# Hybrid encoder block on one core: the last group's two pairs of heads interleaved, their outputs staged in other tiles, modulation sums and FFN scalings placed sooner

## The chip, the cores and the metric

The kernel runs on one core of one Trainium2 chip, as one program. The metric is the device time of one execution in microseconds; the time before is the median of three runs. A core has TensorE (PE in the profile; PEld is its weight load), VectorE (DVE), ScalarE (ACT), GpSimd (POOL) and SyncE (SP). SP, ACT and POOL issue the DMAs.

## The reference

One layer of a bidirectional hybrid block on 256 tokens of width 2048, in fp32, and a final RMSNorm:

```python
mod = silu(c) @ ada_w + ada_b            # shift, scale, gate for the mixer (m) and for the FFN (f)
h   = rms_norm(x) * (1 + scale_m) + shift_m
proj = h @ w_in                          # all branches' inputs
h_a = mLSTM, both directions             # 4 heads, dk 256, dv 512
y_a = (sigmoid(a_o) * rms_norm(h_a)) @ w_branch_a
o_b = gated delta rule, both directions  # 16 heads of 128, behind a conv and l2 norms
y_b = (rms_norm(o_b) * silu(b_z)) @ w_branch_b
x = x + gate_m * ((g_a * y_a + g_b * y_b) @ w_out)
hf = rms_norm(x) * (1 + scale_f) + shift_f
x = x + gate_f * ((silu(gate) * up) @ w_down)     # gate, up = split(hf @ w_gate_up)
out = rms_norm(x) * norm_final_w
```

## The kernel before

Every weight matmul is done with operands split in a high and a low part (three products). ACT makes the high part (`wh`, L171 and L197), DVE the low part (`wl`, L172 and L198). `fjob` (out block of 128 channels) and `tjob` (tile of 512 channels, both token tiles t = 0 and 1) are generators; each `yield` ends a *piece* of 24 or 12 matmuls. The planner of the framework orders the instructions of each engine by its own cost estimates, with program order as priority; an instruction in `order(...)` keeps its place among its engine's instructions.

**Delta-rule stage.** The 16 heads are four groups g of four. For a group, `gdn_phase1` prepares each head, `gdn_invert` and `gdn_blocks` the triangular inverses, and `gdn_phase2(g, p)` finishes a pair p of heads in nine steps, each ended by `yield`: p1 (L717), p2 (L726), p3 (L739), p4 (L751), pa (L763/764, scaled by ACT into `z`), pb (L775, with `r` on DVE), pc (L763/764), po (L785 to L790, with the norm `gdn_norm`: squares on ACT L809, root L813, scaling into `on` on DVE L819), px (transposes of `on`, L796). At the end ACT copies px into `obt` (L798) and sends it to DRAM (`ob_d`, L799). `z` and `r` have one buffer, `on` and `pt` two. Between steps the loop draws pieces of other projections, by `fill` from the list `fills` (value and output gates `v`/`o`, the q and k blocks `a`, merge gates `ma`/`mb`), and for the next heads by `stream`. In group 3 no next heads are left, so every piece is a `fill`; `last` says how many follow each step. 23 pieces are left when the first pair of group 3 begins.

The tiles of this stage lie in the pool `bk`, among them `obt`. The pool `evp` holds evicted tiles of projections: `ev` and `evf` (two buffers of 128 x 256; `keep_f`, L339/L340, stores q and k blocks through it).

**What follows group 3.** `sx.close()` frees `bk`; in its place come `obh`/`obl` (the split delta outputs, L932/L933) and the pool `ml` of the mLSTM: per head the loads `mkq`, `vt`, `sgo` and `bc` on POOL (L937 to L944), and the last group's outputs (`o_load`, L886, POOL), which read `ob_d`. `psc` (L957) is the first matmul of an mLSTM head, `pden` (L981) and `ph` (L1002) follow. `y_b`'s first two pieces (`acc_yb`) use the first group's `obh`; its next two splits are held in program order behind the last group's.

**Modulation sums.** `ada_part` loads 1 MB of `ada_w` on SP (L126) and reduces it on DVE (L127); sixteen such sums and an addition (L129) make one part. `sums()` draws them from the list `background`; `pump()`, called once for every two pieces of a tile job, draws one for every `every[0]` calls. Parts 2, 3 and 4 run through the delta stage up to the output projection `o` (tiles g = 0 to 3), whose loop draws a sum after the listed pieces.

**FFN entry.** The last output tile is finished by token tile: `residual` (L1113 multiply and L1114 add on DVE, L1115 square on ACT), `token_rstd` (L1123, L1124, L1125). `normed(q, t, ...)` scales quarter q of token tile t into `xn` (L1191 on DVE, L1193 on ACT; two buffers of tag `sg`), `moved(b)` transposes block b (`pxn`, L1200), applies scale and shift (`hf`, L1204/L1206) and makes the high part (L1207), `low(b)` the low part (L1210). A loop over pairs of blocks alternates these with pieces of the first gate tile (`gt0`), twelve matmuls a pair of blocks.

Of the kernel before, what the change touches and what calls it, by code (L numbers as in the profile page):

```python
# [9 lines left out]
F32 = mybir.dt.float32  # L10
F32R = mybir.dt.float32r
AF = mybir.ActivationFunctionType
ALU = mybir.AluOpType
PSUM = bass.MemoryType.PSUM

P = 128
T = 256
# [35 lines left out]
def hybrid_block(ctx: ExitStack, tc: tile.TileContext, xr, nfr, crow, pk_d, cst_d, ada2, ada4, win0, winb, wint, wba, wbb, wo, wgu, wd, out, dbg=None):  # L53
    nc = tc.nc
    V, S, G, PE = nc.vector, nc.scalar, nc.gpsimd, nc.tensor

    def pool(stack, name, bufs=1, **kw):
        return stack.enter_context(tc.tile_pool(name=name, bufs=bufs, **kw))
# [27 lines left out]
    def order(ins, yes=True):  # L86

        return tc.keep_in_program_order(ins) if yes else ins
# [58 lines left out]
    count, every = [0], [0]  # L147
# [97 lines left out]
    def run(job):  # L245
        for _ in job:
            pass
# [3 lines left out]
    def fill(n=1):  # L251

        while n and fills:
            if next(fills[0], None):
                n -= 1
            else:
                fills.pop(0)
# [22 lines left out]
    evp = pool(sa, "evp", side="right")  # L280
# [3 lines left out]
    heads, parts = {}, {}  # L284
# [58 lines left out]
    def z_job(g, early=0):  # L343
        def done(ps):
            szs[g] = evp.tile([P, 2, 512], F32, tag="sz", bufs=1, name=f"sz{g}")
            for t in range(2):
                S.activation(szs[g][:, t], ps[t], AF.Silu)
        return tjob(f"z{g}", [wint[g, u] for u in range(4)], hh, hl, done, early)

    def b_job(h, j):  # L350
        return fjob(f"b{h}_{j}", winb[3 * (h - GRP) + j], lambda ps: gdn_conv(h, j, ps))
# [191 lines left out]
    bk = pool(sx, "bk")  # L543
# [161 lines left out]
    def gdn_phase2(g, p):  # L705
# [87 lines left out]
        for e, on in enumerate(ons):  # L793
            h, hl_ = 4 * g + 2 * p + e, 2 * p + e
            for t in range(2):
                PE.transpose(px[:, (2 * e + t) * P : (2 * e + t + 1) * P], on[:, t], ident)  # L796
            obt = bk.tile([P, T], F32, tag="obt", bufs=2, name=f"obt{h}")
            S.activation(obt, px[:, e * T : (e + 1) * T], AF.Copy, scale=pk[:, PK_GNW + h : PK_GNW + h + 1])  # L798
            S.dma_start(ob_d[g][hl_], obt)  # L799
        yield  # L800
# [35 lines left out]
    def stream(h0):  # L836

        todo = []

        def piece():  # L840

            for q in list(todo):
                q[0] -= 1
                if not q[0]:
                    todo.remove(q)
                    next(heads1[q[1]])

        for h in range(h0, min(h0 + 2, NH_B)):
            for j in range(3):
                for _ in b_job(h, j):  # L850
                    piece()
                    yield True
            todo += [[2, h], [4, h]]
        while todo:
            fill(1)
            piece()
            yield True
        while True:
            fill(1)
            yield True  # L860

    heads1 = {h: gdn_phase1(h) for h in range(NH_B)}
    after = (0, 1, 2, 1, 2, 2, 2, 2, 4, 0)
    last = (0, 1, 2, 1, 2, 2, 1, 1, 3, 0)


    for pair in ((0, 1), (2, 3)):
# [9 lines left out]
    def invert(g):  # L877
        gen = gdn_invert(g)
        next(gen)
        fill(4)  # L880
        for _ in gen:
            fill(1)

    def o_load(g, where, bufs):
        o4 = where.tile([P, 4, T], F32, tag="o4", bufs=bufs, name=f"o4_{g}")
        G.dma_start(o4, ob_d[g].rearrange("h p t -> p h t"))  # L886
        return o4

    o4s = []
    invert(0)  # L890
    for g in range(4):
        if g == 3:
            sf.close()
            op = pool(so, "op", side="right")
        blocks = gdn_blocks(g)
        next(blocks)
        fill(8)
        next(blocks)
        fill(1)
        pairs = [gdn_phase2(g, p) for p in range(2)]  # L900
        every[0] = (0, 2, 2, 2)[g]
        for p in range(2):
            pieces = stream(4 * g + 2 * p + 4)
            if g == 3:
                o4s += [o_load(i, op, 3) for i in ((0, 1), (2,))[p]]
            for n in range(1, 10):
                next(pairs[p], None)
                if p == 0:
                    next(blocks, None)
                for _ in range(after[n] if g < 3 else last[n]):  # L910
                    next(pieces)
            for _ in pairs[p]:
                pass

            if g < 3:
                while 4 * g + 2 * p + 5 not in heads:
                    next(pieces)
        if g < 3:
            fills.insert(0, z_job(g + 1))
            every[0] = 0  # L920
            invert(g + 1)
# [114 lines left out]
    def y_a(g, mgh, mgl):  # L1036
        gt = ml.tile([P, 2, 512], F32, tag="gt", bufs=2, name=f"gta{g}")
        nc.sync.dma_start(gt, ma_d[g])

        def done(ps):  # L1040
            c = slice(g * 512, (g + 1) * 512)
            for t in range(2):
                V.scalar_tensor_tensor(gt[:, t], gt[:, t], 1.0, ps[t], ALU.add, ALU.mult)
                V.tensor_tensor(mg[:, t, c], mg[:, t, c], gt[:, t], ALU.add)
            for e2 in range(2):
                px = gps(f"pxm{g}_{e2}")
                for e in range(2):
                    f = 2 * e2 + e
                    for t in range(2):
                        PE.transpose(  # L1050
                            px[:, e * T + t * P : e * T + (t + 1) * P], mg[:, t, g * 512 + f * P : g * 512 + (f + 1) * P], ident
                        )
                b = 4 * g + 2 * e2
                split(mgh[:, b : b + 2], mgl[:, b : b + 2], px.rearrange("p (e t) -> p e t", e=2))
        return tjob(f"ya{g}", [wba[g, u] for u in range(4)], hah, hal, done)
# [32 lines left out]
    mgh, mgl = big(bigC, F32R, "mgh"), big(bigC, F32R, "mgl")  # L1088
    for g in range(4):
        if g == 3:  # L1090
            every[0] = 0
            while len(background) > 2:
                sums()
            row_store(2, ml, 0.5)
        run(y_a(g, mgh, mgl))
    sm_.close()


# [29 lines left out]
    rs1 = xp.tile([P, 3], F32, name="rs1")  # L1128
# [23 lines left out]
    for g in range(4):  # L1152
        def done_o(*a, g=g):
            for t, ps in [a] if g == 3 else enumerate(a[0]):
                residual(t, g, ps, gm, ss1, wp, g == 3)
                if g == 3:
                    token_rstd(ss1, rs1, t)

        if g == 3:
            root()  # L1160
        between = (lambda: next(gt0)) if g == 3 else None
        for i, _ in enumerate(tjob(f"o{g}", [wo[g, u] for u in range(4)], mgh, mgl, done_o, by_token=between)):
            if i in ((4, 6, 7), (1, 2, 4, 6), (1, 2, 4, 6), (1, 2, 4))[g]:
                sums()
            if g == 3 and i == 4:
                sums(P)
                V.scalar_tensor_tensor(
                    affn, mod[:, 4 * KB : 5 * KB], 1.0, pk[:, PK_NFFN : PK_NFFN + KB], ALU.add, ALU.mult
                )
# [16 lines left out]
    def normed(q, t, parts, eng):  # L1186
        if q not in xns:
            xns[q] = hp.tile([P, 2, 512], F32, tag="sg", bufs=2, name=f"xn{q}")
        o, i = xns[q][:, t, parts], x1[:, t, q * 512 + parts.start : q * 512 + parts.stop]
        if eng is V:  # L1190
            order(V.tensor_scalar(o, i, rs1[:, t : t + 1], None, ALU.mult))  # L1191
        else:
            order(S.activation(o, i, AF.Copy, scale=rs1[:, t : t + 1]))  # L1193

    def moved(b):

        px = gps(f"pxn{b}")
        for t in range(2):
            f = b % 4 * P
            order(PE.transpose(px[:, t * P : (t + 1) * P], xns[b // 4][:, t, f : f + P], ident))  # L1200
        hfs[b] = hp.tile([P, T], F32, tag="hf", bufs=2, name=f"hf{b}")
        f, m = affn[:, b : b + 1], mod[:, 3 * KB + b : 3 * KB + b + 1]
        if b % 2 and b > 2:
            order(S.activation(hfs[b], px[:, 0:T], AF.Identity, scale=f, bias=m))  # L1204
        else:
            order(V.tensor_scalar(hfs[b], px[:, 0:T], f, m, ALU.mult, ALU.add))  # L1206
        order(S.activation(hfh[:, b], hfs[b], AF.Copy))  # L1207
# [5 lines left out]
    normed(0, 1, slice(0, 256), V)  # L1213
    for t in range(2):
        normed(0, t, slice(256, 512), S)
    moved(0)
    moved(1)
    low(0)
# [4 lines left out]
    for b in range(2, KB, 2):  # L1223

        next(gt0)
        low(b)
        low(b + 1)
        next(gt0)
        if b % 4 == 2 and b < 12:
            for t in range(2):  # L1230
                normed(b // 4 + 1, t, slice(0, 512), S)
        for e in (b + 2, b + 3):
            if e < KB:
                moved(e)
# [3 lines left out]
    for j in range(FB // 4):  # L1238
# [4 lines left out]
        for e2 in range(2):  # L1243
            px = gps(f"pxf{j}_{e2}")
            for e in range(2):
                f = 2 * e2 + e
                for t in range(2):
                    PE.transpose(px[:, e * T + t * P : e * T + (t + 1) * P], sg[:, t, f * P : (f + 1) * P], ident)
            b = 4 * j + 2 * e2
# [144 lines left out]
```

## Time and profile before

| | before |
|---|---|
| median of 3 runs | 1982.52 us (1982.24 to 1983.56) |
| profiled execution | 1979.27 us, span 1977.3 us |
| PE busy / PEld busy | 1918.9 us (97%) / 1705.5 us |
| DVE / ACT / POOL busy | 1402.5 / 1022.7 / 96.9 us |
| mean granted TensorE clock | 0.988 |
| DMA | 487.76 MB, mean 247 GB/s |

Times inside the profile are microseconds from the first instruction of the span. A row of the timeline gives start, length, engine, source line, operation, what it writes and reads, shapes, how many instructions were merged, and in brackets the idle time of the engine before it with what ended it. An engine name with a q is its queue issuing a DMA. The slices of the page cut the span into 40 parts of 49.4 us.

### The profile page before, as it was taken

To read this page: it belongs to the slowest core of one execution; us is meant where nothing else is said; L and a number is where in the kernel's file an instruction comes from. 1 tells how busy PE (TensorE), PEld (TensorE's weight loads), DVE (VectorE), ACT (ScalarE), POOL (GpSimd) and SP (SyncE) were. 2 spreads that over 40 slices of the span, in tenths; PEclk is the share of its full clock that TensorE was granted. 3 is DMA by queue.
4 is the path that set the end of the run, shared out by engine and by line. 5 is a ranking of instruction groups with operands and counts; after the bars stand their busy time and mean duration, and the time that the engine had idled before them with its cause. 6 is when DMAs were issued, how large, how long until landed. Compare 5 with 4: busy or idle time off the path is not lost.

```text
span 1977.3 us, 27036 instructions
## 1 busy us (share of the span) xinstructions
PE 1918.9 (97%) x10352; PEld 1705.5 (86%) x10352; DVE 1402.5 (71%) x2091; ACT 1022.7 (52%) x1568; POOL 96.9 (5%) x185
## 2 busy tenths in 40 slices
PE   8999999999999999999799999799999999999997
PEld 6887889989989998998688888688888888888886
DVE  5779887878988996965587769766666655555554
ACT  3146657855765686465454444554444444444443
POOL 0000300110100011000200000000000000000000
PEclk9999999999999999999799999899999999999999
DMA  9996665567667765885677679466766765566563
GB/s 400 420 383 194 222 223 192 167 203 283 228 199 247 281 214 191 310 303 190 234 291 266 249 288 419 182 234 235 265 244 237 262 246 193 205 240 203 202 206 114
DMA packets 78675, 487.76 MB, mean 247 GB/s; under 512 B 10265, under 2 KB 15681, under 8 KB 23889
## 3 DMA queue, kind: packets, MB, share of 16 engines
q1 hardware_dynamic: 63360, 450.95, 62.2%
q0 software_dynamic: 7872, 19.99, 4.4%
q10 hardware_dynamic: 7314, 15.10, 2.1%
q8 instruction: 81, 1.33, 0.3%
q14 instruction: 48, 0.39, 0.1%
HBM read 469.16 MB, written 16.83 MB: 246 GB/s over the span
## 4 chain that ended last, share of the span: by engine, by line
PE 73%; DVE 11%; DMA 9%; ACT 4%; issue 2%; POOL 0%; SPq 0%; ACTq 0%; DVEq 0%; POOLq 0%
DMA ra<-ada 5%; PE acc_up L215 4%; PE acc_up L218 4%; PE acc_up L216 4%; PE acc_d L216 4%; PE acc_d L215 4%; PE acc_d L218 4%; PE acc_gt L216 4%; PE acc_gt L215 4%; PE acc_gt L218 4%; PE acc_o L218 2%; PE acc_o L216 2%; PE acc_o L215 2%; PE acc_a L175 2%; PE acc_b L175 2%
## 5 line engine op out<-in xcount | busy, mean ns | idle before, releaser
L198 DVE TENSOR_TENSOR wl_d<-raw_d,wh_d 128x1024 fp32r<-128x1024 f32 x88 | 107.8, 1225 | 102.7 <-ACT wh_d L197 102.7
L127 DVE SCALAR_TENSOR_TENSOR ada<-ada,crow 128x2048 f32<-128x2048 f32 x64 | 146.5, 2289 | 43.6 <-DMA ada<-ada 43.5
L198 DVE TENSOR_TENSOR wl_up<-raw_up,wh_up 128x1024 fp32r<-128x1024 f32 x88 | 107.5, 1225 | 95.9 <-ACT wh_up L197 95.9
L197 ACT ACTIVATE wh_d<-raw_d 128x1024 fp32r<-128x1024 f32 x88 | 93.0, 1057 | 130.5 <-PE acc_d L216 125.3
L198 DVE TENSOR_TENSOR wl_gt<-raw_gt,wh_gt 128x1024 fp32r<-128x1024 f32 x88 | 107.7, 1224 | 72.4 <-ACT wh_gt L197 68.2
L197 ACT ACTIVATE wh_gt<-raw_gt 128x1024 fp32r<-128x1024 f32 x88 | 92.9, 1056 | 120.7 <-PE acc_gt L216 73.2
L197 ACT ACTIVATE wh_up<-raw_up 128x1024 fp32r<-128x1024 f32 x88 | 93.0, 1056 | 118.2 <-PE acc_up L216 71.7
L215 PE MATMUL acc_gt<-wh_gt,hfh 128*128 128x512 f32 x352 | 135.2, 384 | 0.0
L216 PE MATMUL acc_gt<-wh_gt,hfl 128*128 128x512 f32 x352 | 134.6, 382 | 0.0
L175 PE MATMUL acc_b<-hh,wh_b 128*128 128x256 f32 x576 | 134.6, 276 | 0.0
L175 PE MATMUL acc_b<-hl,wh_b 128*128 128x256 f32 x576 | 134.6, 277 | 0.0
L215 PE MATMUL acc_up<-wh_up,hfh 128*128 128x512 f32 x352 | 133.5, 379 | 0.0
L216 PE MATMUL acc_up<-wh_up,hfl 128*128 128x512 f32 x352 | 133.5, 379 | 0.0
L216 PE MATMUL acc_d<-wh_d,ffl 128*128 128x512 f32 x344 | 130.4, 379 | 0.0
L215 PE MATMUL acc_d<-wh_d,ffh 128*128 128x512 f32 x344 | 130.4, 379 | 0.0
L530 PE MATMUL first<-x,raw 128*128 128x256 f32 x512 | 114.5, 382 | 7.5 <-ACT x L523 6.8
L530 PEld LDWEIGHTS first<-x,raw 128*128 128x128 f32 x512 | 96.1, 190 | 25.9 <-ACT x L523 12.4
L175 PEld LDWEIGHTS acc_b<-hl,wh_b 128*128 128x128 f32 x576 | 110.6, 192 | 0.4
L175 PEld LDWEIGHTS acc_b<-hh,wh_b 128*128 128x128 f32 x576 | 110.5, 192 | 0.5
L197 ACT ACTIVATE wh_o<-raw_o 128x1024 fp32r<-128x1024 f32 x64 | 67.1, 1054 | 58.9 <-PE acc_o L216 35.5
L218 PE MATMUL acc_gt<-wl_gt,hfh 128*128 128x512 f32 x352 | 95.3, 385 | 0.0
L171 ACT ACTIVATE wh_b<-raw_b 128x1024 fp32r<-128x1024 f32 x72 | 76.1, 1058 | 37.1 <-PE acc_b L175 22.8
(384 smaller groups left out, 5018.4 us busy)
## 6 DMA issues: line engine op xcount, KB each, us to landing
ada<-ada SPq DMA_DIRECT2D x64, 1024.0 KB, 5.8
raw_gt<-wgu SPq DMA_DIRECT2D x44, 1024.0 KB, 5.0
raw_up<-wgu SPq DMA_DIRECT2D x44, 1024.0 KB, 4.9
raw_d<-wd SPq DMA_DIRECT2D x44, 1024.0 KB, 4.9
raw_b<-winb SPq DMA_DIRECT2D x36, 1024.0 KB, 5.0
ra<-ada SPq DMA_DIRECT2D x32, 1025.0 KB, 15.8
raw<-win SPq DMA_DIRECT2D x16, 1024.0 KB, 17.1
raw_z<-wint SPq DMA_DIRECT2D x16, 1024.0 KB, 5.2
```

The lines of the kernel that those rows point to most:

```text
L127: V.scalar_tensor_tensor(raw, raw, 1.0, row_c[:, :D], ALU.mult, ALU.mult, accum_out=mod[:, c0 + b : c0 + b + 1])
L171: S.activation(wh, raw[:, k0 : k0 + 8], AF.Copy)
L175: PE.matmul(o, wh[:, k], both(x, k0 + k).rearrange("p a b -> p b a"), start=k0 + k + i == 0, stop=False)
L197: order(S.activation(wh, raws[u][:, k0 : k0 + 2], AF.Copy), hold)
L198: order(V.tensor_tensor(wl, raws[u][:, k0 : k0 + 2], wh.bitcast(F32), ALU.subtract), hold)
L215: order(PE.matmul(ps[t], tok(xh, kk, t), turns(wh[:, k]), start=kk == 0, stop=False), early and steps > 1)
L216: PE.matmul(ps[t], tok(xl, kk, t), turns(wh[:, k]), start=False, stop=False)
L218: PE.matmul(ps[t], tok(xh, kk, t), turns(wl[:, k]), start=False, stop=kk == last)
L530: PE.matmul(first[o], raw[:, o], x[:, b], start=b == 0 and o % 2 == 0, stop=b == KB - 1 and o % 2 == 1)
```

## The change

- The outputs `obt` of all groups lie in `evp` under the tag `evf`, which they share with the q and k blocks, and no longer in `bk`.
- In group 3 the two pairs run in one loop of 13 steps: the first pair takes a step in each up to its end, the second from the fifth on, and two pieces are drawn in every step. Groups 0 to 2 run as before.
- `every[0] = 0` moves from the start of the last `y_a` tile to its end, so the counter draws sums there too. The `o` tiles draw 4, 4, 4 and 0 sums instead of 3, 4, 4 and 3.
- `normed` can also run on POOL. The second quarter is scaled there, ahead of the first transposes; the third and fourth are scaled on ACT at b = 4 and 8 instead of b = 6 and 10 (the second was at b = 2).

```diff
-            obt = bk.tile([P, T], F32, tag="obt", bufs=2, name=f"obt{h}")
+            obt = evp.tile([P, T], F32, tag="evf", bufs=2, name=f"obt{h}")
...
-    last = (0, 1, 2, 1, 2, 2, 1, 1, 3, 0)
...
-        for p in range(2):
+        for p in range(2) if g < 3 else ():
             pieces = stream(4 * g + 2 * p + 4)
-            if g == 3:
-                o4s += [o_load(i, op, 3) for i in ((0, 1), (2,))[p]]
...
-                for _ in range(after[n] if g < 3 else last[n]):
+                for _ in range(after[n]):
                     next(pieces)
...
+        if g == 3:
+            flow = [stream(4 * g + 4 + 2 * p) for p in range(2)]
+            for n in range(1, 14):
+                next(pairs[0], None)
+                if n > 4:
+                    next(pairs[1], None)
+                if n < 6:
+                    next(blocks, None)
+                if g == 3 and n in (1, 6):
+                    o4s += [o_load(i, op, 3) for i in ((0, 1), (2,))[n > 1]]
...
+                for _ in range(2):
+                    next(flow[n > 8])
...
     for g in range(4):
         if g == 3:
-            every[0] = 0
             while len(background) > 2:
                 sums()
             row_store(2, ml, 0.5)
         run(y_a(g, mgh, mgl))
+    every[0] = 0
...
-            if i in ((4, 6, 7), (1, 2, 4, 6), (1, 2, 4, 6), (1, 2, 4))[g]:
+            if i in ((2, 4, 6, 7), (1, 3, 5, 7), (1, 3, 5, 7), ())[g]:
                 sums()
...
-        if eng is V:
-            order(V.tensor_scalar(o, i, rs1[:, t : t + 1], None, ALU.mult))
+        if eng is not S:
+            order(eng.tensor_scalar(o, i, rs1[:, t : t + 1], None, ALU.mult))
...
+    for t in range(2):
+        normed(1, t, slice(0, 512), G)
     moved(0)
...
-        if b % 4 == 2 and b < 12:
+        if b % 4 == 0 and b < 12:
             for t in range(2):
                 normed(b // 4 + 1, t, slice(0, 512), S)
```

More of the change, by code (lines that the diff above doesn't have):

```diff
@@ L913, in hybrid_block @@
                 pass
-            if g < 3:
-                while 4 * g + 2 * p + 5 not in heads:
-                    next(pieces)
+            while 4 * g + 2 * p + 5 not in heads:
+                next(pieces)
+        if g == 3:
[8 more added lines that the diff above has]
+                    o4s += [o_load(i, op, 3) for i in ((0, 1), (2,))[n > 1]]
+                if n == 9 and g < 3:
+                    while 4 * g + 5 not in heads:
+                        next(flow[0])
+                for _ in range(2):
+                    next(flow[n > 8])
+            for pair in pairs:
+                for _ in pair:
+                    pass
+            while g < 3 and 4 * g + 7 not in heads:
+                next(flow[1])
         if g < 3:
```

## The prediction

> **What bounds the kernel now.** I read the page first, its busy shares and its slices.
>
> ```profile
> span 1977.3 us, 27036 instructions
> PE 1918.9 (97%) x10352; PEld 1705.5 (86%) x10352; DVE 1402.5 (71%) x2091; ACT 1022.7 (52%) x1568; POOL 96.9 (5%) x185
> PE   8999999999999999999799999799999999999997
> PEclk9999999999999999999799999899999999999999
> ```
>
> TensorE bounds: 58 us of the span are not its work, and the slices show two dips inside the kernel, one near 950 us and one near 1250 us; at both the granted clock dips too. Next the waits of TensorE, which say what ended them (total, times, longest):
>
> ```profile
> PE pxn L1200 <- ACT xn L1193: 11.6, 7, 6.8
> PE psc L957 <- DMA mkq<-kq_d: 3.7, 2, 3.3
> PE acc_yb L215 <- ACT obh L932: 3.5, 1, 3.5
> PE px L796 <- DVE on L819: 3.5, 2, 3.3
> PE pa L764 <- DVE UL L753: 2.8, 3, 1.2
> PE pb L775 <- DVE r L776: 2.3, 1, 2.3
> PE po L786 <- ACT z L768: 0.7, 1, 0.7
> PE px L796 <- ACT obt L798: 0.6, 1, 0.6
> ```
>
> All but the pa row lie in the two places that the diff edits: the end of the last group's second pair with what follows it, and the normalised activations of the FFN. The busy times by stage place them (columns: stretch, length, busy PE, PEld, DVE, ACT, POOL, granted clock, DMA share, GB/s):
>
> ```profile
> 858.00:932.30 74.30, 74.30 (x496) 69.33 (x495) 42.99 (x50) 45.31 (x86) 0.00 (x0) 1.00 0.67 237
> 932.30:946.00 13.70, 7.63 (x56) 6.84 (x54) 4.94 (x9) 7.28 (x21) 0.00 (x0) 1.00 0.55 193
> 966.50:980.10 13.60, 13.11 (x44) 11.31 (x43) 7.18 (x19) 6.20 (x10) 2.00 (x4) 0.50 0.47 158
> 1134.00:1169.00 35.00, 35.00 (x172) 30.83 (x171) 22.40 (x23) 15.52 (x18) 0.51 (x1) 1.00 0.65 228
> 1176.00:1225.00 49.00, 48.49 (x229) 42.26 (x228) 43.26 (x43) 22.94 (x29) 0.00 (x0) 1.00 1.01 420
> 1277.10:1280.50 3.40, 3.40 (x10) 2.65 (x9) 1.92 (x4) 2.23 (x4) 0.00 (x0) 0.50 0.00 0
> ```
>
> Up to 932.3 TensorE never idles in group 3: projection pieces cover both pairs. After it the pieces are gone, and the second pair's tail stands bare.
>
> **Part 1: the second pair four steps behind the first.** No arithmetic changes. The loop asks for 26 pieces (13 per pair before, 2 at each of 13 steps after), but only 23 are left: 7 of the last output gate, 8 of the last q/k blocks, 8 of the last merge gate. Before, the second pair had 10 of them, and by program order the last stood behind its step pc. The timeline shows how they went:
>
> ```profile
> 933.83 1.03 PE L218 MATMUL acc_ma<-wl_ma,hh 128*128 128x512 f32 x4
> 937.56 0.68 PE L775 MATMUL pb<-z,gg 128*128 128x128 f32 x4 [2.26 <-DVE r L776]
> 940.18 0.49 PE L786 MATMUL po<-z,at 128*128 128x128 f32 x2 [0.71 <-ACT z L768]
> 946.25 0.73 PE L796 MATMUL px<-cst,on 128*128 128x128 f32 x2 [3.34 <-DVE on L819]
> 947.54 0.69 PE L796 MATMUL px<-cst,on 128*128 128x128 f32 x2 [0.56 <-ACT obt L798]
> 948.77 0.33 ACTq L799 DMA_DIRECT2D ob_d<-obt  x1
> 950.66 2.95 ACT L932 ACTIVATE obh<-o 128x1024 fp32r<-128x1024 f32 x3 [1.92 <-DMA ob_d<-obt]
> 951.38 0.80 POOL L886 DMA_DIRECT2D o<-ob_d  x1 [100.38 <-DMA ob_d<-obt]
> 952.18 0.76 POOL L937 DMA_DIRECT2D mkq<-kq_d  x1
> 965.24 2.20 PE L957 MATMUL psc<-mkq 128*128 128x256 f32 x7 [3.33 <-DMA mkq<-kq_d]
> ```
>
> The last piece ended at 934.86, as pb began: two pieces earlier than in program order, so TensorE takes pieces ahead whenever a chain step is not ready. The bare tail holds 2.26 + 0.71 + 3.34 + 0.56 = 6.87 us of idle. Afterwards the pieces stretch, by program order, to one behind the second pair's po. If they again run two pieces ahead, the last one stands behind pc: the waits before pb and po go (2.97), the waits for the norm and for obt stay. I take **3.0**; ends 0 (they run out as early as now) and 6.9 (all covered). The total TensorE work is the same, so what is gained is idle time alone. Cover for the moved steps: the row 858 to 932.3, ACT 61% and DVE 58% busy. The two chains share z and r (one buffer each): the second pair's pa comes one step behind the first's po, so the wait falls away in program order. The two loads of earlier outputs stay at about the same pieces.
>
> **Part 2: obt in the evf tiles.** SP's gate load, ACT's obh and POOL's loads all started between 950.66 and 951.38, right after the last ob_d transfer landed: obt lay in the pool whose room obh, mkq, vt and the other tiles take. Without it the room is free when px has read on, at 948.23. obh and yb come up to 2.4 us earlier, but that alone is worth nothing, since TensorE then waits for mkq, and it is those landings that set psc, the decay products and the ph matmuls. POOL's load of the last outputs still needs ob_d. If POOL's later loads pass it, mkq issues at about 948.3 instead of 952.18: 3.9. If they stay behind it: 0. I take **3.2**, near the upper end, because the planned order lets ready work pass waiting work (here pieces passed pb). The load of the last outputs is then late next, by some four POOL issues (0.76 each); its user, yb's second chunk, is held far behind anyway. In the other direction obt can now wait for a q/k eviction's landing in the two evf buffers, with ACT's splits queued behind:
>
> ```profile
> kq_d<-ev_a ACTq DMA_DIRECT2D x4, 128.0 KB, 2.8
> ob_d<-obt ACTq DMA_DIRECT2D x4, 128.0 KB, 1.7
> ```
>
> One wait of at most 2.8 us on ACT, partly hidden by the split buffers: **-0.3**, ends -2.8 and 0. For groups 0 to 2 I count nothing, since the split buffers hide it; with that cover gone it is the same 2.8 us at most, once for each pair.
>
> **Part 3: the modulation sums.** Twelve sums are drawn in the first three output tiles and none in the fourth; before, three of 14 fell in the fourth. Two move into the last y_a tile (the counter now stays on there). On SP their loads of 1 MB queue among those of y_a's weights, where the DMA share is 0.65, and two such loads leave the stretch from 1176 on, where it is 1.01. In the last output tile two sums stood between the steps that TensorE waits for:
>
> ```profile
> 1253.12 0.59 PE L241 MATMUL acc_o<-wl_o,mgh 128*128 128x512 f32 x2
> 1251.77 2.28 DVE L127 SCALAR_TENSOR_TENSOR ada<-ada,crow 128x2048 f32<-128x2048 f32 x1
> 1253.98 0.69 DVE L1114 TENSOR_TENSOR x<-x,tmss 128x512 f32<-128x512 f32 x1
> 1257.37 2.28 DVE L127 SCALAR_TENSOR_TENSOR ada<-ada,crow 128x2048 f32<-128x2048 f32 x1
> 1257.48 0.63 ACT L1115 ACTIVATE tmss<-x 128x512 f32<-128x512 f32 x1 [1.54 <-DVE x L1114]
> 1260.51 1.97 PE L1200 MATMUL pxn<-cst,xn 128*128 128x128 f32 x8 [6.79 <-ACT xn L1193]
> 1266.48 1.32 ACT L1193 ACTIVATE xn<-x,rs 128x512 f32<-128x512 f32 x2
> 1275.75 0.33 PE L1200 MATMUL pxn<-cst,xn 128*128 128x128 f32 x1 [1.72 <-ACT xn L1193]
> ```
>
> The last matmul ended at 1253.71. From there, without sums: some 0.2 to start, multiply and add at 0.69 each, the square some 0.75, and then what now lies between the second sum's end (1259.6) and the first transpose (1260.5), 0.9 for the reduction, root, reciprocal and first scaling. That is 1257.0 to 1257.1 instead of 1260.51: **3.4**. Ends 1.4 (only the second sum leaves the path: it ends at 1259.6, the square before it at 1258.2) and 4.6 (both lengths). The two sums in y_a cost **-0.5**, ends -4.6 (both sums ahead of splits, 2.28 each) and 0: in the last y_a tile and on (1134 to 1169) TensorE has no idle and DVE is 64% busy, which hides them; with that cover gone it is their whole length.
>
> **Part 4: the scalings.** The second block of four goes to POOL ahead of the transposes, the third and fourth are issued two blocks sooner. Waits before pxn after the first: 11.6 - 6.8 = 4.8 us. With xn there, the next limit is ACT's queue: two pairs of scalings, 1.32 each, still stand in it ahead of the conversions that the matmuls need. I leave one such pair, 1.3 of the 4.8, as idle: **3.5**, ends 2.2 (both) and 4.8. POOL's scaling is not in the trace; its nearest rows are memsets:
>
> ```profile
> L552 POOL MEMSET cc<- 128x512 f32 x6 | 2.9, 521 | 5.7 <-DMA raw_v<-wint 5.7
> L552 POOL MEMSET UL<- 128x2048 f32 x1 | 1.8, 1795 | 0.0
> ```
>
> I take 1.3 us for one, between 0.52 and 1.8. The second starts at about 1257 and ends by 1258.8 at the latest; its reader comes after eight transposes and twelve matmuls (1.97 for the former, 1.03 for four of the latter), past 1261. So its price is 0. [...]
>
> **The clock.** In 1277.1 to 1280.5 the clock was 0.50 with TensorE busy throughout, behind the 1.72 us wait at 1275.75: half of 3.4, **1.7**, comes back if those waits go; ends 0 and 1.7. For the first transposes I count nothing: a gap of 3.4 us remains, and the 1.72 us wait was enough here. [...]
>
> **Sum.** 3.0 + 3.2 - 0.3 + 3.4 - 0.5 + 3.5 + 1.7 = 14.0 us. The profiled execution took 1979.27 us (span 1977.3), so 1965.3; the median of the runs, 1982.52, is 3.25 above it, and my number for it is **1968.5**.
>
> **Rivals.** *Early exhaustion (B):* the pieces run out as now and POOL's order stays. Group 3 gives nothing; 14.0 - 6.2 = 7.8 remain: 1974.7. For it: pieces already ran two ahead. Against it: now two pieces stand behind every step of the second pair, where one stood behind four of them. *Sums replaced (C):* another unordered DVE operation, a weight split say, takes the sums' place between the residual steps, and the scalings only move their wait: 1.4 + 1.5 instead of 3.4 + 3.5 + 1.7, so 14.0 - 5.7 = 8.3: 1974.2. *Full cover (D):* 6.9 and 3.9 in group 3, and the clock stays up where it was 0.50 from 966.5 to 980.1 (13.11 busy; some 5 us of it in long matmuls comes back): 14.0 + 3.9 + 0.7 + 5 = 23.6: 1958.9. *Slower (E):* with both chains in flight the planned order misjudges them, and TensorE is held at a chain step while ready pieces queue behind. The row of pa shows 1.2 us at the longest in earlier groups; at 13 steps that is 15.6 us, from which the other terms (14.0 - 3.0 = 11.0) are taken: 4.6 slower, 1987.1. It decides from 11.0 / 13 = 0.85 us a step. Against it: the row 858 to 932.3 has no idle with one chain. *Does not do what it says (F):* group 3 and the FFN both find a next waiter of the same length, and only the clock's 1.7 comes: 1980.8.
>
> **Chances.** My forecast 0.47, B 0.18, C 0.12, D 0.10, E 0.06, F 0.07. Below about 0.2% (4 us) a measurement of this kernel can't tell a change from none. Faster: the first four less 0.04 of B and C that would end within that bound, 0.83; same 0.11; slower 0.06. The range leaves out E, F and half of D: 1959 to 1979.
>
> **What would show it.** Group 3: pieces of acc_ma still running behind the second pair's pb; waits before pb and po gone; obh starting within 1 us of the last px; mkq issued ahead of the load of ob_d. FFN: no L127 between the last acc_o and the first pxn, that gap near 3.4 us, POOL's two scalings ended before 1261 on the old scale, no 0.50 stretch behind them. Wrong if L127 or L198 still stands there, if the psc waits grow by what yb gains, or if waits at p, pa or pb appear between 860 and 930.

## The result and the profile after

| | before | after |
|---|---|---|
| median of 5 runs each | 1983.56 us (1982.24 to 1986.4) | 1965.06 us (1961.58 to 1971.78) |
| ratio of times, 95% interval | | 0.9908 (0.9892 to 0.9923) |
| profiled execution, span | 1979.27, 1977.3 us | 1965.06, 1963.2 us |

The change is faster by 18 us (0.9%); the forecast was 1968.5, in a range of 1959 to 1979. The profiled executions differ by 14.2 us: that of before lay below its median, that of after is its median. Four executions among the experiments (two of the kernel before, one each of two changed kernels) took 2868 to 10526 us, in a slow state, and stand in no ratio below. The page of the changed kernel:

```profile
span 1963.2 us, 27039 instructions
...
PE 1915.5 (98%) x10352; PEld 1701.3 (87%) x10352; DVE 1400.6 (71%) x2091; ACT 1021.8 (52%) x1566; POOL 100.2 (5%) x187
...
PE   8999999999999999998999999999999999999997
...
PEclk9999999999999999999999999999999999999999
```

The busy time of every engine is the same within 5 us, so what was gained is waiting and clock: both dips of before, near 950 and near 1250, are gone from the clock's slices. Three rows of the timeline mark the stages, each the first matmul of one: the last branch projection (`acc_ya`), the output projection (`acc_o`) and the last of the FFN's eleven up tiles (`acc_up`). Before:

```profile
1076.19 0.38 PE L215 MATMUL acc_ya<-wh_ya,hah 128*128 128x512 f32 x1
1169.02 0.38 PE L215 MATMUL acc_o<-wh_o,mgh 128*128 128x512 f32 x1
1717.34 0.38 PE L215 MATMUL acc_up<-wh_up,hfh 128*128 128x512 f32 x1
```

After:

```profile
1067.62 0.38 PE L215 MATMUL acc_ya<-wh_ya,hah 128*128 128x512 f32 x1
1161.89 0.38 PE L215 MATMUL acc_o<-wh_o,mgh 128*128 128x512 f32 x1
1703.18 0.38 PE L215 MATMUL acc_up<-wh_up,hfh 128*128 128x512 f32 x1
```

Up to `acc_ya` 8.6 us were won (parts 1 and 2); `acc_ya` itself takes 92.8 and then 94.3 us, 1.4 more (part 3's price); from `acc_o` to `acc_up` 7.0 us were won (parts 3 and 4); behind that nothing. TensorE's waits after:

```profile
PE pxn L1216 <- ACT xn L1209: 3.5, 1, 3.5
PE acc_yb L218 <- DVE wl_yb L198: 3.1, 2, 2.5
...
PE px L796 <- DVE on L819: 2.4, 1, 2.4
...
PE acc_ya L218 <- DVE wl_ya L198: 1.9, 3, 1.1
PE acc_ma L215 <- ACT ev_a L339: 1.5, 1, 1.5
...
PE acc_gt L215 <- ACT hfh L1223: 1.2, 3, 0.4
```

Seven waits before `pxn` (11.6 us) have become one (3.5), those before `psc` (3.7) are down to 0.6, that for `obh` (3.5) is gone, that before `pb` too. New are `acc_ma`, behind ACT's eviction of a q/k block, `acc_yb`, and `acc_gt` behind `hfh`. The end of group 3 in the timeline of the changed kernel:

```profile
918.61 0.49 PE L786 MATMUL po<-z,at 128*128 128x128 f32 x2 [0.72 <-ACT z L768]
...
923.69 0.50 PE L796 MATMUL px<-cst,on 128*128 128x128 f32 x2 [2.35 <-DVE on L819]
...
924.75 0.69 PE L796 MATMUL px<-cst,on 128*128 128x128 f32 x2 [0.56 <-ACT obt L798]
...
926.15 0.81 POOL L953 DMA_DIRECT2D mkq<-kq_d  x1 [72.91 <-ACT obt L798]
...
926.46 0.38 ACT L339 ACTIVATE ev_a<-acc_a 128x256 f32<-128x256 f32 x1 [0.51 <-DMA ob_d<-obt]
...
926.89 0.79 PE L215 MATMUL acc_ma<-wh_ma,hh 128*128 128x512 f32 x1 [1.45 <-ACT ev_a L339]
...
927.45 1.06 ACT L948 ACTIVATE obh<-o 128x1024 fp32r<-128x1024 f32 x1 [0.61 <-ACT ev_a L339]
...
930.61 0.39 ACT L339 ACTIVATE ev_a<-acc_a 128x256 f32<-128x256 f32 x1 [2.10 <-DMA ob_d<-obt]
...
933.36 1.97 PE L973 MATMUL psc<-mkq 128*128 128x256 f32 x8 [0.17 <-issue]
...
936.08 0.76 POOL L885 DMA_DIRECT2D o<-ob_d  x1 [0.86 <-DMA sgo<-o_d]
```

The last px ends at 925.44 (before: 948.23). That is not 23 us gained: the last merge gate (`acc_ma`, 96 matmuls), which ran from 910.18 to 934.86 among the second pair's steps, now runs from 926.89 to 955.04, behind them. Its first matmul waits for an eviction `ev_a`, which frees an accumulator, and the first two of the four `ev_a` wait for landings of `obt`, with which they now share the two evf buffers (the other two, at 933.49 and 938.69, wait for the landings of the first two). The first `ev_a` of these four stood at 888.83 before. The 30 us behind the last px, by busy times (columns as in the prediction's windows), first before, then after:

```profile
948.23:978.23 30.00, 22.26 (x77) 18.07 (x77) 14.49 (x29) 10.92 (x15) 10.77 (x18) 0.67 0.73 254
```

```profile
925.44:955.44 30.00, 27.94 (x119) 23.61 (x120) 21.27 (x30) 17.81 (x22) 10.25 (x17) 0.90 0.97 332
```

TensorE is busy 27.9 us of 30 instead of 22.3, at a mean clock of 0.90 instead of 0.67: the merge gate covers the landings of the mLSTM's loads.

### The profile page after: what moved, and what is told of

Same layout as the page of the kernel before. It is cut to its first block, busy times and chain, and to the rows that moved or that the text cites. A ratio compares the mean times of both kernels' runs of the same rounds, so it can differ in the third digit from the quotient of the medians.

```text
span 1963.2 us, 27039 instructions
## 1 busy us (share of the span) xinstructions
PE 1915.5 (98%) x10352; PEld 1701.3 (87%) x10352; DVE 1400.6 (71%) x2091; ACT 1021.8 (52%) x1566; POOL 100.2 (5%) x187
## 4 chain that ended last, share of the span: by engine, by line
PE 71%; DMA 10%; DVE 10%; issue 4%; ACT 3%; POOL 0%; ACTq 0%; SPq 0%; DVEq 0%; POOLq 0%
PE acc_up L216 4%; PE acc_up L215 4%; PE acc_up L218 4%; PE acc_d L216 4%; PE acc_d L215 4%; PE acc_d L218 4%; PE acc_gt L216 4%; PE acc_gt L215 4%; PE acc_gt L218 4%; DMA ra<-ada 4%; PE acc_b L175 3%; PE acc_o L218 3%; PE acc_o L216 2%; PE acc_o L215 2%; DMA ada<-ada 2%
## 5 line engine op out<-in xcount | busy, mean ns | idle before, releaser
L127 DVE SCALAR_TENSOR_TENSOR ada<-ada,crow 128x2048 f32<-128x2048 f32 x64 | 146.5, 2289 | 56.2 <-DMA ada<-ada 56.1
L197 ACT ACTIVATE wh_o<-raw_o 128x1024 fp32r<-128x1024 f32 x64 | 67.1, 1054 | 57.7 <-PE acc_o L216 34.6
```

Source lines behind the costliest of these rows:

```text
L127: V.scalar_tensor_tensor(raw, raw, 1.0, row_c[:, :D], ALU.mult, ALU.mult, accum_out=mod[:, c0 + b : c0 + b + 1])
L197: order(S.activation(wh, raws[u][:, k0 : k0 + 2], AF.Copy), hold)
```

## The experiments

All ratios are to the kernel before, run beside each on the same chip; 0.001 is 2.0 us. Intervals of ±0.0015 are 3 us, so the difference of two changed kernels is uncertain by some 4 us, and by 5 where the intervals are ±0.0022.

| kernel | ratio (95%) | last px ends | `acc_ma` runs | last `acc_yb` ends |
|---|---|---|---|---|
| before | 1 | 948.2 | 910 to 935 | 1076.4 |
| after | 0.9908 (0.9892 to 0.9923) | 925.4 | 927 to 955 | 1067.8 |
| `obt` in evf alone | 0.9955 (0.9941 to 0.9969) | 936.9 | 917 to 963 | 1068.6 |
| interleaving alone | 0.9977 (0.9965 to 0.999) | 940.2 | 918 to 942 | 1074.6 |
| sums alone | 0.9997 (0.9978 to 1.0015) | 948.9 | 912 to 936 | 1078.9 |
| scalings alone | 0.9974 (0.996 to 0.9988) | 950.2 | 909 to 934 | 1079.2 |
| evf and interleaving | 0.9921 (0.9899 to 0.9942) | 923.6 | 925 to 953 | 1064.3 |
| before, `obt` in ev | 1.0048 (1.003 to 1.0067) | 950.9 | 939 to 962 | 1091.0 |
| after, `obt` in ev | 0.9938 (0.9916 to 0.996) | 945.9 | 923 to 948 | 1079.8 |
| after, head 12 alone in evf | 0.9933 (0.9918 to 0.9949) | 929.8 | 925 to 955 | 1067.0 |
| after, six steps behind | 0.9949 (0.9934 to 0.9964) | 946.3 | 914 to 939 | 1076.5 |
| after, two steps behind | 0.993 (0.9917 to 0.9943) | 925.3 | 928 to 956 | 1070.7 |
| after, scaling on ACT | 0.9899 (0.9877 to 0.9921) | 925.4 | 927 to 955 | 1066.8 |
| after, no sums in the last `y_a` | 0.9903 (0.9885 to 0.9922) | 924.0 | 926 to 954 | 1064.8 |

The times in the last three columns are of one profiled execution each, and such executions of one kernel differ by some us (that with all of `obt` in ev holds a wait of 4.4 us in an earlier group, below); the ratios are over all runs.

**The four parts, each alone.** The first two theories were the prediction's own: theory 1, the interleaving covers the second pair's tail and `obt`'s place matters little; theory 2, the gain is the room that `obt` leaves in `bk`, which lets the mLSTM's loads start at once.

```diff
-            obt = bk.tile([P, T], F32, tag="obt", bufs=2, name=f"obt{h}")
+            obt = evp.tile([P, T], F32, tag="evf", bufs=2, name=f"obt{h}")
```

> The kernel before with obt in the evf tiles and nothing else changed. Theory 1 (the gain in group 3 comes from the two chains ending sooner, with pieces of the last merge gate left behind them to cover the norm and the mLSTM loads): within 2 us of before, since the second chain ends as late as before and mkq's landing is all that can move. Theory 2 (the gain comes from the room of bk being free 2.4 us sooner and the loads passing the one that waits for ob_d): 4 to 8 us faster.

Measured: 0.9955, about 9 us, the largest of the four. Theory 1 missed it. Behind the last px in this kernel:

```profile
936.91:966.91 30.00, 27.47 (x115) 23.31 (x115) 22.30 (x30) 18.23 (x22) 10.25 (x17) 0.89 1.00 363
```

With the old loops, TensorE is as busy there (27.5 us of 30) as in the changed kernel; no wait for `mkq` at `psc` is left. But three of the four `ev_a` also come late, at 939.01, 942.50 and 948.52, which theory 2 does not speak of. A third theory came from this row, *held back*: what counts is that the shared buffers hold the q and k evictions, so that the merge gate's matmuls run behind the last px, where they cover the landings.

```diff
-        for p in range(2):
+        for p in range(2) if g < 3 else ():
...
+                next(pairs[0], None)
+                if n > 4:
+                    next(pairs[1], None)
```

> The kernel before with the two pairs of group 3 in one loop of 13 steps, obt still in bk. Theory 1: 5 to 8 us faster, px of the second pair some 20 us earlier than 948. Theory 2: 0 to 2 us faster, since obt's landing still holds the room.

Measured: 0.9977, some 4.6 us. Here px ends 8 us sooner than before and no step of either pair waits over 0.25 us from 860 on, more than part 1 promised; but behind px the time is given back:

```profile
PE psc L974 <- DMA mkq<-kq_d: 9.1, 2, 7.8
```

```profile
940.15:970.15 30.00, 17.44 (x61) 13.18 (x60) 15.74 (x23) 10.92 (x13) 9.88 (x17) 0.77 0.85 312
```

The merge gate ran among the chains (918 to 942), and TensorE has 17.4 us of work in the next 30. A matmul that fills a gap ahead of px is missing behind it.

```diff
-            every[0] = 0
             while len(background) > 2:
...
-            if i in ((4, 6, 7), (1, 2, 4, 6), (1, 2, 4, 6), (1, 2, 4))[g]:
+            if i in ((2, 4, 6, 7), (1, 3, 5, 7), (1, 3, 5, 7), ())[g]:
```

> The kernel before with the modulation sums moved alone. If the two sums between the residual steps were the price: the gap before the first pxn falls from 6.8 to 3.4 us and the run is 2 to 3.5 us faster, 1 us of it given back in the last y_a tile. If another DVE operation takes their place: within 1 us.

Measured: 0.9997 (0.9978 to 1.0015): not to be told from nothing, nor from the 2 to 3.5 us expected. The first wait of pxn does shrink as forecast (6.79 to 3.38), while `acc_ya` waits 1.9 us for `wl_ya`, where it waited 0.5.

```diff
+    for t in range(2):
+        normed(1, t, slice(0, 512), G)
...
-        if b % 4 == 2 and b < 12:
+        if b % 4 == 0 and b < 12:
```

> The kernel before with the scalings moved alone (second quarter on POOL, third and fourth two blocks sooner). If the waits before pxn were ACT's scalings: the 4.8 us after the first wait fall to about 1.2 and the run is 3 to 5 us faster. If they only move behind hfh: within 1.5 us.

Measured: 0.9974, 5.2 us (2.4 to 7.9). Of pxn's seven waits only the first is left:

```profile
PE pxn L1200 <- ACT xn L1193: 6.9, 1, 6.9
```

**Parts 1 and 2 together.** The edit is both diffs above.

> Parts 1 and 2 together (both pairs of group 3 interleaved, obt in evf), without the new sums and scalings. By themselves they gave ratios of 0.9977 and 0.9955 to the kernel before, and the changed kernel 0.9908. If the parts add, this gives 0.9932 (some 1970.5 us against 1984): px ends at 925 to 926 as in the changed kernel, the stretch from 1250 loses 6.79 us at the first pxn again. If the two parts take the same waits away (both move matmuls of ma3 and the q and k loads against the last pair), it gives no more than evf alone, 0.995 (1974 us).

Measured: 0.9921, and the singles multiply to 0.9932: they add up. px ends at 923.63. All four parts multiply to 0.9903 against 0.9908 measured.

**Room or held back.** The same room in `bk`, but `obt` shares the other buffers of the pool, so `ev_a` is not held.

```diff
-            obt = evp.tile([P, T], F32, tag="evf", bufs=2, name=f"obt{h}")
+            obt = evp.tile([P, 2, 512], F32, tag="ev", bufs=2, name=f"obt{h}")[:, 0, :T]
```

In the kernel before:

> The kernel before with obt in the tiles of tag ev instead of evf: bk is freed as in evf alone, but the four evictions ev_a no longer share slots with obt. Theory room (the gain of evf alone, some 9 us, comes from the q and k loads that no longer wait for the landing of obt): as much here, 1974 to 1976 us, mkq issued within 1 us of the last px. Theory held back (it comes from the evictions ev_a that wait for obt's landings, so that the accumulators stay full and the matmuls of ma3 run behind the last px and cover the waits there): ev_a at 890 to 915 again, acc_ma done at about 935, before the last px, and most of the waits behind px are back: 1980 to 1984 us.

In the changed kernel:

> The changed kernel with obt in the tiles of tag ev instead of evf. The evictions ev_a come early, and the matmuls of ma3 run from about 905 to 930 among the last steps of the pairs: the waits there (0.72 before po, 2.35 before px, 1.45 before acc_ma) are covered. Theory room: nothing is lost behind the last px, since the loads still start there; 3 to 4.5 us less than the changed kernel, ratio to before 0.9885 to 0.9895, 1961 to 1962 us against 1984. Theory held back: the matmuls are missing behind px, psc waits 3 to 8 us for mkq as before the change, and the sum is 0 to 4 us more than the changed kernel, ratio 0.991 to 0.993.

Measured: 1.0048 and 0.9938. Against `obt` in evf that is 18 us more in the old loops (1.0048 against 0.9955) and 6 us more in the new ones (uncertain by some 5; the kernel with the scaling on ACT, below, measured on the same chip and with the changed kernel's group 3, is 8 us below it). POOL's timeline of the first, and TensorE's waits of the second:

```profile
951.64 0.80 POOL L937 DMA_DIRECT2D mkq<-kq_d  x1 [98.92 <-DVE ada L127]
```

```profile
PE psc L973 <- DMA mkq<-kq_d: 9.0, 2, 8.0
...
PE p L717 <- issue: 4.4, 1, 4.4
```

Both kernels issue `mkq` 0.7 us behind the last px (950.93 and 945.86), and `psc` waits 6.6 and 9.0 us all the same. So the room alone, which was part 2's mechanism, does not pay: theory 2 falls. Interleaving, sums and scalings by themselves multiply to 0.9948, and the second kernel, which has the room besides, is at 0.9938: 2 us, inside the uncertainty. In the second kernel nothing of 860 to the last px is idle, and the 30 us behind it are the mirror image:

```profile
946.00:976.00 30.00, 16.74 (x74) 13.61 (x73) 16.33 (x28) 11.54 (x15) 10.26 (x17) 0.84 0.89 320
```

Its second `mkq` (issued at 949.50) takes 17.2 us from issue to landing (13.6 at the longest in the changed kernel). The last split of the merge gate's weights, whose buffer goes to a later weight load of 1 MB, stands there at 938.61, ahead of it; in the changed kernel it stands at 946.06, behind the second `mkq` (929.07), and the next loads of `raw_yb` go out from 944.47 on. That the traffic of such a load is what delays it was not tried by itself. The 4.4 us before p, in an earlier group and for nothing that the profile shows, belong to this execution, the longest of its kernel (1978.0 against a median of 1972.0). The first kernel is not a clean opposite, and held back's own expectation for it missed: its `ev_a` came at 917 to 941, not at 890 to 915, and 44 of the 96 `acc_ma` matmuls still ran behind px. It also has waits of 7.3 us in all between 885 and 906, at steps of the first pair that were covered before, and 1.3 us at 909 before `acc_a`, behind a merge gate's eviction. So only a part of its 18 us can be cover missing behind px. The 6 us of the second are the better measure.

**A part of the matmuls ahead of px.** Head 12's output alone in evf:

```diff
+            if 4 * g + 2 * p + e in (13, 14, 15):
+                obt = evp.tile([P, 2, 512], F32, tag="ev", bufs=2, name=f"obt{h}")[:, 0, :T]
```

> The changed kernel, but of group 3's heads only head 12 keeps obt in evf; heads 13 to 15 take the tiles of tag ev. So ev_a may come one by one between the landings: in the order of the instructions the q and k matmuls of the last two pieces stand among the second pair's last steps, and those of ma3 begin only just ahead of the last px and stay behind it. Theory held back (what counts is that ma3's matmuls, 28 us in the changed kernel, lie behind the last px, under the landing of the q and k loads): that cover is kept, and the waits ahead of px (0.72 before po, 2.35 before px, 1.45 before acc_ma) go: 2 to 4.5 us less than the changed kernel, ratio to before 0.9885 to 0.990. Rival (the chain of the pairs sets px's end, and matmuls put at its end are missing at its start): px ends at 925 to 928 with the same sum of waits, 0.9908. Second rival (as with all obt in ev, traffic of the next weights meets the loads): psc waits over 3 us, 0.992 to 0.994.

Measured: 0.9933, 5 us above the changed kernel: the gain did not come. The `ev_a` came one by one (907 to 925) and 22 of the 96 `acc_ma` matmuls ran ahead of px. Ahead of the last px a wait of 2.6 us is left, at the first pair's px, and 0.5 us at pb, and a wait of 3.1 us for `mkq` appeared at `psc` (landings up to 16.9 us after issue), which is the second rival. The profiled execution of this kernel was its fastest, with the changed kernel's span (1963.4 us), so it does not show all of the 5 us; the rest stays open.

**How far behind.**

```diff
-            for n in range(1, 14):
+            for n in range(1, 16):
...
-                if n > 4:
+                if n > 6:
```

> The changed kernel with the second pair six steps behind the first instead of four. If the gain of the interleaving is that the two chains run side by side, two more steps of the second pair stand alone at the end: px ends 2 to 5 us later than 925.4, and the time is 1 to 4 us more, ratio 0.9915 to 0.993. If only the place of the other matmuls counts (held back behind the last px whatever the lag), no difference from 0.9908.

Measured: 0.9949, 8 us above the changed kernel, twice the expectation. px ends at 946.3, not at 927 to 930. Two `ev_a` now come between the landings (913.53, 919.10), the merge gate starts at 914.02 and is done before the last px, and the old waits return:

```profile
PE acc_yb L215 <- ACT obh L948: 3.9, 1, 3.9
...
PE px L796 <- DVE on L819: 3.4, 1, 3.4
```

`mkq` is issued 0.7 us behind px here too, and `psc` waits only 0.9 us; the waits behind px are at `acc_yb` (3.9) and at `pden` (2.9) instead. So the lag acts through the order of the shared buffers too: with six steps the first pair's outputs have landed by 919.10, long before the second pair's want the buffers (945.08), and q/k evictions slip in between.

> The changed kernel with the second pair two steps behind the first instead of four. In the order of the instructions all matmuls of ma3 stay behind the last px, as with four; the last q and k matmuls now stand up to the second pair's po. Theory held back: the cover behind px is kept, po's wait of 0.72 goes, the norm's 2.35 and the 1.45 ahead of acc_ma stay: px ends at 923 to 926 and the time is 0 to 2 us less than the changed kernel, ratio 0.990 to 0.9908, against six steps, where ma3 ran among the pairs (0.9949). If the lag itself set the time (the two chains contend for DVE and ACT when they are closer), px ends 2 us or more later and the time is 1 to 4 us more: 0.9915 to 0.993.

Measured: 0.993, 4 us above the changed kernel, no more than the uncertainty. Neither forecast fits as a whole: px ends at 925.33 and the merge gate stays behind it (928 to 956), as held back says, po's wait is gone; yet the time is longer, as the rival's number has it. The profiled execution has 2.7 us ahead of `acc_ma` and later 3.5 us at `acc_yb` and 3.3 at `pxa`, both for DVE, and 5.5 at `pxn` (3.5 in the changed kernel), but it was this kernel's longest execution (1976.4 against a median of 1968.7). What the 4 us are, if they are real, is open.

**The last two parts.** The second quarter's scaling at its new place, on ACT:

```diff
-        normed(1, t, slice(0, 512), G)
+        normed(1, t, slice(0, 512), S)
```

> The changed kernel with the two scalings of the second quarter at the same place, on ACT instead of POOL (1.57 and 1.72 us there). If POOL's part matters, ACT has two more scalings of 128x512 (some 1.05 us each) ahead of the evictions for the gates and the first gate's hfh comes later: 0.5 to 2 us more than the changed kernel, ratio 0.991 to 0.992. If only the place in the order matters (the scalings off the wait of the second pxn), no difference: 0.9908 within the interval.

Measured: 0.9899 (0.9877 to 0.9921), no difference that the interval shows: at this place either engine will do. On ACT the two take 0.71 us each, not the 1.05 expected, which was an estimate. That the place alone is the gain was not tried apart from the other scalings.

```diff
         if g == 3:
+            every[0] = 0
             while len(background) > 2:
...
-((2, 4, 6, 7), (1, 3, 5, 7), (1, 3, 5, 7), ())[g]
+((2, 4, 6, 7), (1, 3, 5, 7), (1, 3, 5, 7), (1, 2))[g]
```

> The changed kernel without the two sums in the last y_a job (none are asked for there, as before); two more stand in the last o job after its pieces 1 and 2. If the part of the third edit that counts is the last o job, freed behind its fourth piece, the stalls of acc_ya of the changed kernel (0.29, 1.06 and 0.55) shrink to 0.8 in all as before, the first pxn still waits about 3.5, and the time is 0 to 1.5 us less: ratio 0.990 to 0.991. If the two sums were well placed in y_a, the first pxn waits 5.8 to 6.8 again (two passes of 2.29 us more on DVE ahead of the last residual) and the time is 2 to 3.5 us more: 0.992 to 0.9925.

Measured: 0.9903, no difference either, though its first pxn waits 6.9 us again. What stands at pxn does not stand at `acc_ya`, whose waits fall from 1.9 to 1.3 us: within the uncertainty of some 5 us the sums cost the same in both places. None of these kernels is measurably better than the changed one.

## Why the prediction was right or wrong, point by point

The time came out right, 3.4 us below the number; the sum, 14.0, met the profiles' 14.2 only because wrong terms balanced, which is luck: on the chip parts 1 and 2 are worth 15.7 us (11.5 to 20.0) where 5.9 were forecast, and parts 3 and 4, by their single runs, 5.8 where the forecast had 8.1 with the clock. The 3.25 us added for the median were not needed, since after's profiled execution is its median.

- **Part 1, "if they again run two pieces ahead": the step that failed.** The count of pieces from program order was no help. The matmuls of `acc_ma` are not used up around pc; all 96 run behind the last px. Of the two waits said to go, pb's 2.26 went, po's 0.72 stayed; the norm's 3.34 fell to 2.35. The interleaving alone is worth 4.6 us on the chip (term: 3.0), and by another way: it took all waits away and px came 8 us sooner, of which `psc` took 5.4 back (9.1 against 3.7).
- **Part 2, evf at -0.3: wrong in sign and by far in size.** I priced one wait of 2.8 us on ACT. The wait holds the last four q and k evictions, with them the accumulators and the next 28 us of matmuls: the first `ev_a` at 926.46 instead of 888.83. The order that results is worth some 6 us against `obt` in ev, uncertain by 5, and 8 us against six steps of lag, where `acc_ma` runs ahead of px.
- **Part 2, the early loads at 3.2: what was forecast came, but not its worth.** `mkq` is issued 0.7 us behind px and ahead of the load of the last outputs (926.15, 936.08); the kernels with `obt` in ev show that this alone leaves `psc` waiting 6.6 to 9.0 us. `obh` came 2.0 us behind px, not within 1: ACT's `ev_a` stands ahead of it.
- **Group 3 together:** 5.9 forecast; 8.6 in the profiles up to `acc_ya`, 15.7 on the chip. The 8.6 hold a loss from ahead of group 3: this execution of the changed kernel has a stretch at half clock from 729.90 on, which that of before has not, and came into group 3 1.7 us late (the same `acc_a` matmul at 796.85 and, before, at 795.14).

```profile
729.90:733.31 3.41, 3.41 (x18) 3.41 (x18) 3.41 (x12) 1.89 (x7) 0.00 (x0) 0.50 0.77 238
```

So 10.3 were won from there to `acc_ya`. Idle time accounts for 5.9 (from 860 to 1110, below), the clock for about the rest, and I had left the clock there to rival D alone. Why the chip shows more than these two executions is open.

- **Part 3: mis-sized.** 2.9 forecast; in the profiles 3.3 at pxn less 1.4 in `acc_ya`, 1.9; on the chip not to be told from 0, nor from 2.9 (0.9997, and 0.9903 with the sums moved back). The gap of 3.4 us and its steps came as worked out (3.47, no L127 in it). The cover "no idle and DVE is 64% busy" in the last `y_a` did not hold: `wl_ya` comes just in time there (TensorE waits 1.9 us for it, 0.5 before), and an average does not show that.
- **Part 4 and the clock: right.** 3.5 + 1.7 forecast, 3.7 in the profiles (7.0 less the 3.3), 5.2 (2.4 to 7.9) on the chip. The stretch at 0.50 behind 1277.08 is gone; that right behind the first transposes' gap, for which nothing was counted, stayed (1248.72 to 1255.55; before, 1256.60 to 1263.43). POOL's scalings took more than my 1.3 and stayed inside 0.52 to 1.8:

```profile
1246.61:1292.90 46.29, 41.65 (x188) 34.48 (x189) 31.71 (x47) 31.34 (x52) 3.29 (x2) 0.93 0.46 159
```

```profile
1247.12 1.57 POOL L1207 TENSOR_SCALAR xn<-x,rs 128x512 f32<-128x512 f32 x1 [80.54 <-DVE rs L1141]
...
1249.92 1.72 POOL L1207 TENSOR_SCALAR xn<-x,rs 128x512 f32<-128x512 f32 x1 [1.23 <-DVE rs L1141]
1250.08 1.97 PE L1216 MATMUL pxn<-cst,xn 128*128 128x128 f32 x8 [3.47 <-ACT xn L1209]
```

The first fence is the stretch behind the last output matmul, the second its timeline: TensorE is busy 41.7 of 46.3 us, where before it was 34.6 in as long a stretch:

```profile
1253.71:1300.00 46.29, 34.64 (x157) 28.64 (x157) 29.07 (x50) 28.47 (x51) 0.00 (x0) 0.89 0.34 114
```

POOL's first scaling (1.57 us) shows no extra time against the second (1.72).

- **Rivals.** B held in one point (the tail's norm and po waits stay) and not in POOL's order; C's split between the residual steps did not come; of D, the clock behind px came in part; E's waits at pa did not appear, nor F's next waiters of the same length.

## What to carry to other kernels

Matmuls that a planner may place freely were a stock here that covered one stall only (TensorE was busy 17.4 of the 30 us behind px, at a clock of 0.77, where the merge gate ran ahead of it, and 27.9, at 0.90, where it ran behind): look which of the stalls is longer and has the clock to lose, and ask what holds the stock there; a ring of two small buffers shared by two users can be that. To price a moved tile, list who else takes that ring in program order and what each of them keeps occupied while it waits (here an eviction, its accumulator, and the matmuls behind). Count what stands in front of a gap and behind it together; the interleaving alone won 8 us ahead of px and lost 5.4 of them at `psc` behind it.

## What the runs showed of the clock

I had not expected how little idle time lowers the clock. Its low stretches begin on a grid of 3.41 us: in before, from 860 us on, they start at 945.99, 966.47, 1055.21, 1256.60 and 1277.08 and last 10.24, 13.65, 3.41, 6.83 and 3.41 us, all at 0.50. Stretches of that grid by busy times, before and then after. In 1273.66 and in 1245.30 TensorE is busy 1.42 and 1.31 us, and the stretch behind each is at 0.50:

```profile
1270.25:1273.66 3.41, 3.41 (x20) 2.98 (x18) 2.41 (x4) 1.66 (x3) 0.00 (x0) 1.00 0.28 41
1273.66:1277.08 3.42, 1.42 (x8) 0.84 (x7) 2.04 (x4) 2.61 (x5) 0.00 (x0) 1.00 0.66 273
1277.08:1280.49 3.41, 3.41 (x10) 2.66 (x9) 1.93 (x4) 2.23 (x4) 0.00 (x0) 0.50 0.00 0
...
935.74:939.15 3.41, 1.59 (x13) 1.59 (x14) 2.06 (x5) 0.96 (x2) 0.00 (x0) 1.00 0.66 159
939.15:942.57 3.42, 2.71 (x24) 2.51 (x24) 0.00 (x0) 1.14 (x4) 0.00 (x0) 1.00 0.99 381
```

```profile
1245.30:1248.72 3.42, 1.31 (x7) 0.80 (x5) 1.86 (x5) 1.35 (x4) 1.57 (x1) 1.00 0.00 0
1248.72:1255.55 6.83, 5.47 (x17) 4.45 (x18) 4.18 (x10) 5.29 (x13) 1.72 (x1) 0.50 0.01 2
1255.55:1258.96 3.41, 3.41 (x19) 3.00 (x18) 2.75 (x6) 1.63 (x4) 0.00 (x0) 1.00 0.74 219
```

With 1.59 us busy (935.74) the clock stayed. The stretch at 1273.66 was idle 2.0 us in several gaps, not only for the 1.72 us wait to which the prediction put the low one behind it. In all 14 profiles, from 860 to 1290 us, each of the 43 stretches at full clock with TensorE busy under 45% was followed by a low one; of 24 between 45% and 60%, nine were; of 134 between 60% and 94%, three; of some 1430 busier ones, six. These nine have one thing in common: 14 to 24 of the `pden` matmuls start in them, which are one column wide (128x1) and which the profile counts as busy. In before:

```profile
1051.80:1055.21 3.41, 3.41 (x29) 3.33 (x28) 3.41 (x4) 1.11 (x3) 0.00 (x0) 1.00 0.93 317
1055.21:1058.62 3.41, 3.41 (x10) 2.70 (x9) 0.84 (x7) 0.48 (x1) 0.00 (x0) 0.50 1.02 423
```

The first of these holds 24 `pden` matmuls in 2.7 us. With `pden` counted as idle, 56 of 57 stretches under 45% are followed by a low one, and none of some 1540 over 60%: matmuls this narrow held the clock up no better than idle time here, though no run varied them.

So an idle microsecond near others cost more than itself here: from 860 to 1110 us, before and after,

```profile
860.00:1110.00 250.00, 235.10 (x1239) 207.22 (x1238) 167.81 (x225) 129.62 (x212) 12.37 (x21) 0.95 0.69 247
```

```profile
860.00:1110.00 250.00, 240.98 (x1293) 212.65 (x1292) 175.81 (x236) 135.60 (x221) 12.37 (x21) 0.97 0.71 259
```

TensorE is idle 14.9 and 9.0 us, and the clock rises from 0.95 to 0.97. As an estimate, half of TensorE's busy time inside the low stretches is lost (the `acc_yb` matmuls of before start 0.22 us apart ahead of 1051 and 0.43 us apart behind 1055.3): 11.2 and 6.0 us, two thirds to three quarters of the waits themselves. Idle time and clock together give 11.1 us won, a little more than the 10.3 measured. In group 3 my sum had the first kind only.
